# A two-layer encoder trunk on one core: layer norms with one mean operation, scaled weights, and separate output tiles for the last blocks

## The chip, the cores and the metric

The kernel runs on one core of one Trainium2 chip. The core has a matrix engine (TensorE, PE in the rows, with PEld for its weight loads), a vector engine (VectorE, DVE), a scalar engine (ScalarE, ACT), a general engine (GpSimd, POOL) and an engine that issues most transfers (SyncE, SP). Each takes its own list of instructions; they wait for one another by semaphores. The metric is device microseconds of one execution. Three runs of the kernel before took 2295.4, 2296.66 and 2297.1 us.

## What is computed

Two layers over 1024 rows (tokens) of 1024 numbers in float32. Layer 0 mixes tokens by latent attention, layer 1 by differential attention; each layer then has a gated feed-forward part:

```
h = LN(ALPHA*h + mixer(h))
h = LN(ALPHA*h + (silu(h@Wg) * (h@Wu)) @ Wd)

LN(z) = (z - mean(z)) * (mean((z-mean(z))**2) + 1e-5)**-0.5 * g + b     # per row of 1024
```

With `D = 1024` and `q` the sum of the squared distances from the mean, the norm's factor `(q/D + eps)**-0.5` is `sqrt(D) * (q + D*eps)**-0.5`, and `sqrt(D)` is 32. So the same result comes from the plain sum of squares if `g` holds 32 times its values.

## The kernel before

The rows are worked on in eight blocks of 128 (`tb` 0 to 7), one row per partition. Products are made in split precision: each operand is a high and a low part, and three matrix products replace one. The high part is a cast on ACT, the low part a subtraction on DVE or GpSimd (`split`, L480 and L481; `op_...` are weights so prepared). Inside the feed-forward parts the products are arranged in seven sub-products over halves of the operands instead of eight, which is where the many sums on DVE come from.

The order is as follows: projections and attention of layer 0, its output projection (`out_proj`), feed-forward 0 (`ffn`), projections and attention of layer 1, its output projection (class `OutProj`: begun in the attention, finished by `rest`), feed-forward 1. The instructions stand in the program in one order. A planner in the framework turns them into one list per engine: it simulates the program with costs of its own and gives a free engine the ready instruction that stands earliest in the program. `tc.high_priority(n)` moves a stretch of the program up by n places. `behind(i, j)` fixes that `i` stands after `j` in the list of their engine. The engines then run those lists as they are, so a plan that took a transfer for faster than it is makes the engine wait at that place. Buffers come from pools: the tag `big` has five buffers of 128 x 2 x 1024 numbers, handed out in turn for weights, partial sums and results, and a sixth user waits for one to come free. The tag `small` has 22 little ones for per-row values.

There are 32 layer norms, one for each block at four places, all made by `layer_norm` (L163):

- L166 and L167 (DVE) make minus the mean twice, once divided by 32, from two partial sums of the row.
- L170 (ACT) squares the two halves of `z/32 - mean/32` into a bank that is no longer needed, and adds them up (`ssq`).
- L176 (DVE) writes `y = (z - mean) * g`.
- L178 (DVE) adds the two sums and epsilon, L180 (GpSimd) raises to the power -0.5, and L183 (DVE) writes `y = y*rs + b`, followed by the store to memory (L184).

In most places `y` is `z` itself, so that L176 overwrites what L170 reads and has to wait for it. Only `out_proj` gives its last block a tile of its own:

```python
if tb == LAST_ORDER[-1]:
    y = big_tile(f"y_{nm}", F32)[:, 0]
```

The blocks of the output projections go in the order `LAST_ORDER`, 6 7 4 5 2 3 0 1. After each block's norm, `raw_x` (L440) transposes the block before it on PE (rows `xTp_a`) and makes its operands for the feed-forward part. For the last block that call is `pending()`, which `ffn` makes under `high_priority(40)` after its first gate products (`ga`). These, and the preparing of their weights (`op_gp` from `gp`, later `op_g` from `gr`), come after `rest` in the program and fill PE around that place.

The weights `g` and `b` of a norm are loaded once for a place, spread to all partitions, by transfers that GpSimd issues: `mg` and `mb` in `out_proj`, `gb` in `rest` (L424), `fg` and `fb` in `ffn` (L152), and for blocks 0 to 3 of feed-forward 0 a second pair `gb_f` (L896). They reach the queue long before the first norm that uses them.

At the end of feed-forward 1, the eleven steps of the last sub-product ("t4") run for blocks 0 and 1 together, then for 2, then for 3 (`dw` rows on PE). `last(t)` adds a finished bank to `z` (L811) and norms it; `banks_read` lists the adds. The norm of block 3 writes its last line in two halves. Blocks 4 to 7 have been normed earlier (`finish(4 + t, ...)`).

Of the kernel before, what the change touches and what calls it, by code (L numbers as in the profile page):

```python
# [9 lines left out]
F32 = mybir.dt.float32  # L10
F32R = mybir.dt.float32r
AF = mybir.ActivationFunctionType
ALU = mybir.AluOpType
# [3 lines left out]
P = 128  # L17
S = 1024
D = 1024
# [11 lines left out]
LN_EPS = 1e-5  # L31
# [11 lines left out]
def trunk(  # L43
# [66 lines left out]
    def big_tile(name, dt=F32R):  # L110
        return big.tile([P, 2, 1024], dt, tag="big", name=name)
# [13 lines left out]
    def small(name, n=1):  # L125
        return sp.tile([P, 2], F32, tag="small", name=name, bufs=22)[:, :n]
# [35 lines left out]

    def layer_norm(z, sums, junk, y, g, b, name, dst, n=1):  # L163

        nmu = small(f"nmu_{name}", 2)
        V.tensor_scalar(nmu[:, 0:1], sums[:, 0:1], sums[:, 1:2], -1.0 / (32 * D), ALU.add, ALU.mult)  # L166
        V.tensor_scalar(nmu[:, 1:2], sums[:, 0:1], sums[:, 1:2], -1.0 / D, ALU.add, ALU.mult)  # L167
        ssq = small(f"ssq_{name}", 2)
        squares = [
            A.activation(  # L170
                junk[i], z[:, i * 512:(i + 1) * 512], AF.Square,
                bias=nmu[:, 0:1], scale=1.0 / 32, accum_out=ssq[:, i:i + 1],
            )
            for i in range(2)
        ]
        centred = V.scalar_tensor_tensor(y, z, nmu[:, 1:2], g, ALU.add, ALU.mult)  # L176
        ve = small(f"ve_{name}")
        V.tensor_scalar(ve, ssq[:, 0:1], ssq[:, 1:2], LN_EPS, ALU.add, ALU.add)  # L178
        rs = small(f"rs_{name}")
        scaled = G.tensor_tensor(rs, ve, mhalf[:, 0:1], ALU.pow)  # L180
        for i in range(n):
            c = slice(i * D // n, (i + 1) * D // n)
            V.scalar_tensor_tensor(y[:, c], y[:, c], rs, b[:, c], ALU.mult, ALU.add)  # L183
            nc.sync.dma_start(dst[:, c], y[:, c])  # L184
        return squares[0].ins, centred.ins, scaled.ins

    def to_xT(y, xT, tb, name, where):
        hf, c = tb // 4, (tb % 4) * P
# [89 lines left out]
    def out_proj(side, w_o, o_dram, x_src, x_dst, lng, lnb, xo):  # L278


        with tc.tile_pool(name="op0", bufs=2, side=side, reuse_waits="tile") as pool:
            g = bcast_row(pool, lng, D, "mg0", "g")
            b = bcast_row(pool, lnb, D, "mb0", "b")
            wo = []
            for h in range(H):
                dst = ()
                if h in (0, 1, 2, 3, 7):
                    t = big_tile(f"wo0_{h}")
                    dst = (t[:, 0], t[:, 1])
                elif h == 6:  # L290
                    t = pool.tile([P, 2, D], F32R, tag=f"wo{h}", name=f"wo0_{h}", bufs=1)
                    dst = (t[:, 0], t[:, 1])
                wo.append(load_w(w_o[h], 1024, f"wo0_{h}", *dst))
            prev = None
            for tb in LAST_ORDER:
                nm = f"a0_{tb}"
                of = pool.tile([P, H, P], F32, tag="of", name=f"of_{nm}", bufs=2)
                src = o_dram[tb // 2][:, :, (tb % 2) * P:(tb % 2) * P + P]
                nc.sync.dma_start(of, src.rearrange("h p q -> p h q"))
                ot = pool.tile([P, 2, D], F32R, tag="oh", name=f"oh_{nm}").rearrange("p a (h q) -> p a h q", h=H)  # L300
                oh, ol = ot[:, 0], ot[:, 1]
                A.copy(oh, of)
# [14 lines left out]
                if tb == LAST_ORDER[-1]:  # L317
                    y = big_tile(f"y_{nm}", F32)[:, 0]
                layer_norm(z, sums, junk, y, g, b, nm, x_dst[tb * P:(tb + 1) * P, :])
                if prev is not None:  # L320
                    raw_x(prev[1], xo, prev[0], f"a0_{prev[0]}")
                prev = (tb, y)
        return lambda: raw_x(prev[1], xo, prev[0], f"a0_{prev[0]}")

    class OutProj:
# [95 lines left out]
        def rest(self, lng, lnb, xo):  # L421
            gb = big_tile("gb1", F32)
            for i, src in enumerate((lng, lnb)):
                nc.gpsimd.dma_start(gb[:, i], src.partition_broadcast(P))  # L424
            prev = None
            for tb in LAST_ORDER:
                if tb not in LAST_ORDER[:2]:
                    self.of(tb)
                if tb != LAST_ORDER[0]:
                    self.late(tb)  # L430
                z = self.z[tb]
                layer_norm(z, self.sums[tb], [self.m[tb, nh] for nh in range(2)], z, gb[:, 0], gb[:, 1],
                           f"a1_{tb}", self.x_dst[tb * P:(tb + 1) * P, :])
                if prev is not None:
                    raw_x(self.z[prev], xo, prev, f"a1_{prev}")
                prev = tb
            self.st.close()
            return lambda: raw_x(self.z[prev], xo, prev, f"a1_{prev}")

    def raw_x(y, xo, tb, name):  # L440

# [55 lines left out]
    def ffn(side, xo, xst, pending, layer, x_src, x_dst, lng, lnb, next_x, spare=()):  # L497
# [365 lines left out]

        x4 = accumulators("v", "x")
        whole(x4, from_h(6, "3"), block(1, hi_half, "b22"), True)
        for t in range(4):
            added(0, hi_half, x4[t], t, 1)
            finish(4 + t, [x4[t], x4[t]])
# [4 lines left out]

        def last(t):
            added(1, lo_half, y4[t], t, 0)
            finish(t, [y4[t], y4[t]])

        new, rest, normed = None, [], []
        if next_x is None:
            hs, ws = [], []  # L880
# [618 lines left out]
```

## Time and profile before

| | us |
|---|---|
| median of three runs | 2296.66 |
| profiled execution | 2296.31 |
| span of its instructions | 2294.4 |
| PE busy | 2249.9 (98%) |
| DVE busy | 1562.8 (68%) |
| ACT busy | 1017.9 (44%) |
| GpSimd busy | 864.8 (38%) |
| transfers, mean of 16 engines | 33.6% on the queue that SP issues to |

A row of the timeline has start, duration, engine, line, operation, output<-inputs by the program's names without buffer numbers, shape, count, and in brackets the idle time ahead of it and who ended it. A row of the waits has total, times and longest. Where the rows are the busy times of a stretch, they have each engine's busy time with the number of instructions in brackets, then the clock that PE was granted, the share of transfer time and the rate. `L183` is line 183 of the kernel. A matrix product's end is modelled, so the time from start to start (0.23 us for 512 columns here) says more than its duration.

### The profile page before, as it was taken

How to read it: one execution, taken by the hardware profiler on the slowest of the kernel's cores; microseconds unless marked ns; L12 is line 12 of the kernel's file. 1: busy time of each engine (PE TensorE's matmuls, PEld its weight loads, DVE VectorE, ACT ScalarE, POOL GpSimd, SP SyncE). 2: the span in 40 equal slices, each digit the busy share in tenths (PEclk: the TensorE clock that was granted, in tenths of full speed). 3: DMA queues.
4: the chain of work that ended last, by engine and by line, in shares of the span. 5: the costliest groups of instructions: out<-in, count | busy, mean ns of one | idle time of the engine just before them, and what ended most of it. 6: DMA issues, size and time to landing. Idle time of an engine off the chain costs nothing.

```text
span 2294.4 us, 31183 instructions
## 1 busy us (share of the span) xinstructions
PE 2249.9 (98%) x11410; PEld 1915.7 (83%) x11410; DVE 1562.8 (68%) x2899; ACT 1017.9 (44%) x2096; POOL 864.8 (38%) x688
## 2 busy tenths in 40 slices
PE   8999999999999999999999999999999999999997
PEld 8899997878888887888888888987778888887886
DVE  5667664696666668667476667676677666658777
ACT  4455573342333334445465656555432233324353
POOL 2232241114444445555432424221014444436564
PEclk9999999999999999999999999999999999999999
DMA  5010125334435338454310212054244232337353
GB/s 201 14 34 31 41 72 181 136 130 145 177 132 198 125 114 326 184 188 156 102 47 24 66 37 70 19 211 144 96 170 154 72 125 82 130 123 304 141 205 121
DMA packets 105545, 288.28 MB, mean 126 GB/s; under 512 B 7968, under 2 KB 30112, under 8 KB 94896
## 3 DMA queue, kind: packets, MB, share of 16 engines
q1 hardware_dynamic: 100976, 275.87, 33.6%
q0 software_dynamic: 4416, 10.42, 1.6%
q8 instruction: 90, 1.47, 0.3%
q14 instruction: 63, 0.52, 0.1%
HBM read 205.00 MB, written 77.07 MB: 123 GB/s over the span
## 4 chain that ended last, share of the span: by engine, by line
PE 88%; DVE 6%; DMA 3%; issue 2%; ACT 1%; POOL 1%; SPq 0%; DVEq 0%; POOLq 0%; ACTq 0%
PE gb L526 14%; PE gc L526 10%; PE ga L526 10%; PE dw L795 6%; PE zp_a L394 4%; PE s_a L216 4%; PE s_b L216 3%; PE dx L795 3%; PE dv L795 3%; PE bp L143 3%; PE bp L144 3%; PE bp L145 3%; PE dy L795 3%; PE o_a L255 2%; PE o_b L255 2%
## 5 line engine op out<-in xcount | busy, mean ns | idle before, releaser
L480 ACT CAST op_g<-gr 128x512 fp32r<-128x512 f32 x240 | 146.9, 621 | 370.8 <-PE gb L526 183.3
L481 POOL TENSOR_TENSOR op_g<-gr,op_g 128x512 fp32r<-128x512 f32 x104 | 146.4, 1413 | 248.2 <-ACT op_g L480 142.7
L481 DVE TENSOR_TENSOR op_h<-rh,op_h 128x512 fp32r<-128x512 f32 x154 | 163.8, 1091 | 63.4 <-ACT op_h L480 63.4
L526 PE MATMUL ga<-xh_m,op_g 128*128 128x512 f32 x512 | 168.1, 389 | 0.0
L480 ACT CAST op_h<-rh 128x512 fp32r<-128x512 f32 x154 | 92.9, 619 | 136.6 <-PE dx L795 36.1
L795 PE MATMUL dw<-op_w_t,op_h 128*128 128x512 f32 x660 | 151.4, 390 | 0.1
L795 PEld LDWEIGHTS dw<-op_w_t,op_h 128*128 128x128 f32 x660 | 123.6, 188 | 26.0 <-DVE op_h L481 0.5
L222 ACT ACTIVATE l_b<-l_b,mx_b 128x256 f32<-128x256 f32 (+7 forms) x128 | 99.5, 778 | 79.7 <-DVE mx_b L219 77.6
L1303 POOL TENSOR_SCALAR l_b<-l_b,r_b,cst 128x128 f32<-128x128 f32 (+3 forms) x64 | 52.8, 825 | 204.6 <-DVE r_b L224 194.0
L795 PE MATMUL dx<-op_w_b,op_h 128*128 128x512 f32 x528 | 122.2, 391 | 6.8 <-ACT op_w_b L480 3.9
L481 POOL TENSOR_TENSOR op_w_t<-tt,op_w_t 128x512 fp32r<-128x512 f32 x66 | 98.6, 1497 | 79.6 <-ACT op_w_t L480 77.8
L795 PEld LDWEIGHTS dx<-op_w_b,op_h 128*128 128x128 f32 x528 | 98.6, 188 | 30.1 <-ACT op_w_b L480 4.7
L481 DVE TENSOR_TENSOR op_g<-gr,op_g 128x512 fp32r<-128x512 f32 x136 | 110.8, 819 | 15.6 <-ACT op_g L480 15.3
L526 PE MATMUL gb<-t4h_f,op_g 128*128 128x512 f32 x352 | 115.9, 390 | 3.4 <-DVE tmp L609 3.4
L481 POOL TENSOR_TENSOR op_g<-s,op_g 128x512 fp32r<-128x512 f32 x40 | 54.3, 1358 | 167.9 <-ACT op_g L480 159.6
L526 PE MATMUL gb<-t2h_f,op_g 128*128 128x512 f32 x352 | 115.6, 390 | 0.4 <-DVE op_g L481 0.4
L526 PE MATMUL gc<-t1h_f,op_g 128*128 128x512 f32 x352 | 115.4, 389 | 0.0
L526 PE MATMUL gc<-b22h_f,op_g 128*128 128x512 f32 x352 | 115.3, 389 | 0.0
L526 PE MATMUL gb<-t3h_f,op_g 128*128 128x512 f32 x352 | 115.2, 389 | 0.0
L526 PEld LDWEIGHTS ga<-xh_m,op_g 128*128 128x128 f32 x512 | 96.1, 188 | 19.9
L143 PE MATMUL bp<-xT_f,h_wb 128*128 128x512 f32 x256 | 103.0, 402 | 0.0
L145 PE MATMUL bp<-xT_f,l_wb 128*128 128x512 f32 x256 | 101.6, 397 | 0.0
(378 smaller groups left out, 6753.9 us busy)
## 6 DMA issues: line engine op xcount, KB each, us to landing
gr<-in_w_gu SPq DMA_DIRECT2D x44, 1024.0 KB, 6.9
rh<-h_dr SPq DMA_DIRECT2D x28, 1024.0 KB, 4.8
h_dr<-sh SPq DMA_DIRECT2D x22, 1024.0 KB, 5.1
h_dr<-hp SPq DMA_DIRECT2D x22, 768.0 KB, 4.1
tt<-in_w_dn SPq DMA_DIRECT2D x22, 512.0 KB, 7.9
rh<-h_dr SPq DMA_DIRECT2D x14, 768.0 KB, 4.3
wo_dr<-op_pwo SPq DMA_DIRECT2D x16, 512.0 KB, 3.4
z<-xs_dr SPq DMA_DIRECT2D x16, 512.0 KB, 10.0
```

Of the source, the lines that this page charges most:

```text
L143: T.matmul(ps_out, lh, rh, start=(i == 0), stop=False)
L144: T.matmul(ps_out, lh, rl, start=False, stop=False)
L145: T.matmul(ps_out, ll, rh, start=False, stop=(i == n - 1))
L216: T.matmul(s[:, :w], lh, rh[:, ks], start=(j == 0), stop=(j == len(q_pass) - 1))
L222: A.activation(l[:, :n], l[:, :n], AF.Exp, bias=mx, scale=-1.0, accum_out=sm)
L255: T.matmul(po[:, c], a, b[:, j % 2, c], start=st, stop=sp_, skip_group_check=True)
L394: T.matmul(m, a[:, h, :], self.wo[h][w][:, c], start=(start and h == heads[0] and a is oh and w == 0), stop=(stop and h == heads[-1] and a ...
L480: A.copy(hi, src)
L481: return eng.tensor_tensor(lo, src, f32(hi), ALU.subtract).ins
L526: T.matmul(o, w[:, a, kc], x[b][:, k, :], start=(first and k == 0 and (a, b) == (0, 0)), stop=(k == 3 and a == 1), skip_group_check=True,)
L795: T.matmul(o, h[:, a, c], w[:, b_], start=(first and (a, b_) == (0, 0)), stop=(last and a == 1), skip_group_check=True,)
L1303: G.tensor_scalar(l1[:, :n], l1[:, :n], r1, nlam, ALU.mult, ALU.mult)
```

## The change

Three things are changed.

1. In `layer_norm` the mean is made once, undivided by 32. The squares are of `z - mean`, epsilon is multiplied by 1024, and `g` must hold 32 times its values: the new `scale_g` multiplies it in place on ACT (128 x 1024), once at each of the four places where a `g` is loaded. In the program this stands ahead of the first norm there. `layer_norm` also returns its last DVE instruction.
2. In `rest` the last block (1) writes its norm into a `big` tile of its own, and the whole norm of that block stands under `high_priority(40)`. `raw_x` reads that tile.
3. At the end of feed-forward 1 the last four blocks write their norms into two `big` tiles, two blocks each. For blocks 2 and 3, the add of the finished bank to `z` is fixed behind the last DVE instruction of the norm before it.

```diff
     def layer_norm(z, sums, junk, y, g, b, name, dst, n=1):
 
-        nmu = small(f"nmu_{name}", 2)
-        V.tensor_scalar(nmu[:, 0:1], sums[:, 0:1], sums[:, 1:2], -1.0 / (32 * D), ALU.add, ALU.mult)
-        V.tensor_scalar(nmu[:, 1:2], sums[:, 0:1], sums[:, 1:2], -1.0 / D, ALU.add, ALU.mult)
+        nmu = small(f"nmu_{name}")
+        V.tensor_scalar(nmu, sums[:, 0:1], sums[:, 1:2], -1.0 / D, ALU.add, ALU.mult)
         ssq = small(f"ssq_{name}", 2)
         squares = [
             A.activation(
                 junk[i], z[:, i * 512:(i + 1) * 512], AF.Square,
-                bias=nmu[:, 0:1], scale=1.0 / 32, accum_out=ssq[:, i:i + 1],
+                bias=nmu, scale=1.0, accum_out=ssq[:, i:i + 1],
             )
             for i in range(2)
         ]
-        centred = V.scalar_tensor_tensor(y, z, nmu[:, 1:2], g, ALU.add, ALU.mult)
+        centred = V.scalar_tensor_tensor(y, z, nmu, g, ALU.add, ALU.mult)
         ve = small(f"ve_{name}")
-        V.tensor_scalar(ve, ssq[:, 0:1], ssq[:, 1:2], LN_EPS, ALU.add, ALU.add)
+        V.tensor_scalar(ve, ssq[:, 0:1], ssq[:, 1:2], D * LN_EPS, ALU.add, ALU.add)
...
-            V.scalar_tensor_tensor(y[:, c], y[:, c], rs, b[:, c], ALU.mult, ALU.add)
+            done = V.scalar_tensor_tensor(y[:, c], y[:, c], rs, b[:, c], ALU.mult, ALU.add)
             nc.sync.dma_start(dst[:, c], y[:, c])
-        return squares[0].ins, centred.ins, scaled.ins
+        return squares[0].ins, centred.ins, scaled.ins, done.ins
+
+    def scale_g(g):
+        A.activation(g, g, AF.Copy, scale=float(math.sqrt(D)))
...
# out_proj
+                if prev is None:
+                    scale_g(g)
                 layer_norm(z, sums, junk, y, g, b, nm, x_dst[tb * P:(tb + 1) * P, :])
...
# OutProj.rest
-                z = self.z[tb]
-                layer_norm(z, self.sums[tb], [self.m[tb, nh] for nh in range(2)], z, gb[:, 0], gb[:, 1],
-                           f"a1_{tb}", self.x_dst[tb * P:(tb + 1) * P, :])
+                z = y = self.z[tb]
+                last = tb == LAST_ORDER[-1]
+                if prev is None:
+                    scale_g(gb[:, 0])
+                if last:
+                    y = big_tile(f"y_a1_{tb}", F32)[:, 0]
+                with tc.high_priority(40 if last else 0):
+                    layer_norm(z, self.sums[tb], [self.m[tb, nh] for nh in range(2)], y, gb[:, 0], gb[:, 1],
+                               f"a1_{tb}", self.x_dst[tb * P:(tb + 1) * P, :])
                 if prev is not None:
-                    raw_x(self.z[prev], xo, prev, f"a1_{prev}")
-                prev = tb
+                    raw_x(prev[1], xo, prev[0], f"a1_{prev[0]}")
+                prev = (tb, y)
...
# ffn
         whole(x4, from_h(6, "3"), block(1, hi_half, "b22"), True)
+        scale_g(g)
         for t in range(4):
...
         def last(t):
             added(1, lo_half, y4[t], t, 0)
-            finish(t, [y4[t], y4[t]])
+            if t % 2 == 0:
+                ys.append(big_tile(f"y_{nm}_{t}", F32))
+            if t > 1:
+                behind(banks_read[-1], normed[-1][3])
+            normed.append(finish(t, [y4[t], y4[t]], ys[-1][:, t % 2]))
...
+            scale_g(gb[:, 0])
             whole(y4, from_h(2, "4", ("o",)), t4(), False)
```

More of the change, by code (lines that the diff above doesn't have):

```diff
@@ L430, in rest @@
                     self.late(tb)
-                z = self.z[tb]
-                layer_norm(z, self.sums[tb], [self.m[tb, nh] for nh in range(2)], z, gb[:, 0], gb[:, 1],
-                           f"a1_{tb}", self.x_dst[tb * P:(tb + 1) * P, :])
+                z = y = self.z[tb]
[7 more added lines that the diff above has]
+                               f"a1_{tb}", self.x_dst[tb * P:(tb + 1) * P, :])
                 if prev is not None:
-                    raw_x(self.z[prev], xo, prev, f"a1_{prev}")
-                prev = tb
+                    raw_x(prev[1], xo, prev[0], f"a1_{prev[0]}")
+                prev = (tb, y)
             self.st.close()
-            return lambda: raw_x(self.z[prev], xo, prev, f"a1_{prev}")
+            return lambda: raw_x(prev[1], xo, prev[0], f"a1_{prev[0]}")
     def raw_x(y, xo, tb, name):
@@ L875, in last @@
             added(1, lo_half, y4[t], t, 0)
-            finish(t, [y4[t], y4[t]])
+            if t % 2 == 0:
[3 more added lines that the diff above has]
+            normed.append(finish(t, [y4[t], y4[t]], ys[-1][:, t % 2]))
         new, rest, normed = None, [], []
         if next_x is None:
-            hs, ws = [], []
+            hs, ws, ys = [], [], []
             for h, w in zip(from_h(2, "4", late=True), t4()):
```

## The prediction

> **What bounds the kernel now.** I read the page first: busy shares and the chain that ended last.
>
> ```profile
> span 2294.4 us, 31183 instructions
> ...
> PE 2249.9 (98%) x11410; PEld 1915.7 (83%) x11410; DVE 1562.8 (68%) x2899; ACT 1017.9 (44%) x2096; POOL 864.8 (38%) x688
> ...
> PE 88%; DVE 6%; DMA 3%; issue 2%; ACT 1%; POOL 1%; SPq 0%; DVEq 0%; POOLq 0%; ACTq 0%
> ```
>
> TensorE (PE) is busy for 2249.9 of 2294.4 us and is 88% of the chain. No layer norm can give back more than PE's idle 44.5 us, and only the part of it that a norm causes. The profiled execution took 2296.31 us (1.9 us lie around its span), 0.35 us below the median of the runs, 2296.66. So I next read who makes PE wait.
>
> ```profile
> PE xTp_a L148 <- DVE z_a L183: 2.1, 1, 2.1
> ...
> PE xTp_f L148 <- DVE y_f L183: 0.8, 1, 0.8
> ```
>
> (Columns: total us, times, longest.) Of all of PE's waits these two alone name a norm's last line, L183. The first belongs to the last block of `OutProj.rest`, which the change edits. What it costs beside the wait is in the busy times by stretch (PE first; PEclk is the granted clock, third from the end):
>
> ```profile
> core 0: us, PE busy (x) PEld busy (x) DVE busy (x) ACT busy (x) POOL busy (x), PEclk, DMA share, GB/s
> 353.00:357.00 4.00, 4.00 (x13) 3.32 (x13) 1.23 (x1) 2.13 (x4) 0.00 (x0) 0.51 1.04 399
> ...
> 1644.00:1646.70 2.70, 0.64 (x3) 0.19 (x1) 2.26 (x5) 1.59 (x3) 0.93 (x1) 1.00 0.80 256
> 1646.70:1651.00 4.30, 4.27 (x16) 3.70 (x17) 1.96 (x3) 2.10 (x5) 0.00 (x0) 0.60 1.01 390
> ```
>
> After the wait PE ran 4.30 us at a granted clock of 0.60, which is 0.40 x 4.30 = 1.72 us lost behind it. The wait is worth 2.09 + 1.72 = 3.81 us.
>
> **The change, part by part.**
>
> *One mean operation.* 32 norms (two per layer, eight blocks each) lose L167, a 0.2 us instruction that follows L166 by 0.12 us (the two rows at 1639.56 and 1639.68 below). That is 3.8 us of VectorE (DVE) in all, hidden where PE is busy; cover gone, it counts 0.12 us per exposed norm. I take 0.1 us at the second wait above; in the two chains below it is already left out.
>
> *The wait in `rest`.* The timeline of its last block, all engines:
>
> ```profile
> 1639.56 0.20 DVE L166 TENSOR_SCALAR nmu_a<-sum_a 128x1 f32<-128x1 f32 x1
> 1639.68 0.21 DVE L167 TENSOR_SCALAR nmu_a<-sum_a 128x1 f32<-128x1 f32 x1
> 1639.80 2.02 DVE L481 TENSOR_TENSOR op_gp<-gp,op_gp 128x512 fp32r<-128x512 f32 x2
> ...
> 1641.34 0.19 ACT L170 ACTIVATION_READ_ACCUMULATOR zp_a<-z_a,nmu_a 128x1 f32 x1
> ...
> 1642.95 1.27 DVE L176 SCALAR_TENSOR_TENSOR z_a<-z_a,nmu_a,gb 128x1024 f32<-128x1024 f32 x1
> 1644.15 0.20 DVE L178 TENSOR_SCALAR ve_a<-ssq_a 128x1 f32<-128x1 f32 x1
> ...
> 1645.39 1.29 DVE L183 SCALAR_TENSOR_TENSOR z_a<-z_a,rs_a,gb 128x1024 f32<-128x1024 f32 x1 [0.44 <-POOL rs_a L180]
> ...
> 1646.73 1.61 PE L148 MATMUL xTp_a<-ident,z_a 128*128 128x128 f32 x8 [2.09 <-DVE z_a L183]
> ...
> 1647.52 0.69 DVE L459 TENSOR_TENSOR xr_m<-xTp_a,xr_m 128x512 f32<-128x512 f32 x1 [0.25 <-PE xTp_a L148]
> ...
> 1649.55 0.69 DVE L481 TENSOR_TENSOR op_gp<-gp,op_gp 128x512 fp32r<-128x512 f32 x1 [1.33 <-ACT op_gp L480]
> ...
> 1651.29 0.69 DVE L557 TENSOR_TENSOR gr<-gr 128x512 f32<-128x512 f32 x1 [1.05 <-DMA gr<-in_w_gu]
> ```
>
> In place, L176 cannot overwrite `z` while ScalarE's (ACT's) squares read it; meanwhile DVE takes other work (2.02 us of `op_gp`, two adds of `raw_x`), so L178 comes 2.6 us after the squares end (1641.53 against 1644.15). With `y` in its own tile and 40 places of priority L176 follows L166 at once (to about 1641), and L178 waits only for the squares: 1641.55, or 0.67 later behind one foreign operation. L178 to L183 took 1.24, L183 takes 1.29: done at 1644.1 to 1644.7. PE's work ahead of the transposes ends at 2.09 before 1646.73, that is 1644.64. The wait shrinks to at most 0.1. What is late next: DVE's first `gr` work, which waits for a DMA until 1651.29. Nothing in the change brings that load sooner; the new tile even takes one of the five `big` buffers, and a load that wants one may have to wait for it. Ends: nothing gained (DVE's following stretch stays pinned to that load, and PE meets it later) and 3.81 gained. I take the DVE idle time that the earlier norm can fill before that load, 0.25 + 1.33 + 1.05 = 2.63 (its three waits between 1646.6 and 1651.3): **-2.6 us**.
>
> *The clock rule.* The row above gives 0.60 after 2.09 us of waiting. [...]
>
> *The end.* The last four blocks, from the timeline:
>
> ```profile
> 2269.75 12.85 PE L795 MATMUL dw<-wt,op_h 128*128 128x512 f32 x55 [0.73 <-POOL wt L481]
> ...
> 2273.80 0.69 DVE L811 SCALAR_TENSOR_TENSOR z<-z,dw 128x512 f32<-128x512 f32 x1
> ...
> 2277.56 0.21 DVE L178 TENSOR_SCALAR ve_f<-ssq_f 128x1 f32<-128x1 f32 x1
> ...
> 2278.28 0.21 DVE L166 TENSOR_SCALAR nmu_f<-fs 128x1 f32<-128x1 f32 x1
> ...
> 2283.51 0.68 DVE L811 SCALAR_TENSOR_TENSOR z<-z,dw 128x512 f32<-128x512 f32 x1
> ...
> 2284.11 1.28 DVE L176 SCALAR_TENSOR_TENSOR z<-z,nmu_f,fg 128x1024 f32<-128x1024 f32 x1
> ...
> 2285.43 0.20 DVE L166 TENSOR_SCALAR nmu_f<-fs 128x1 f32<-128x1 f32 x1
> ...
> 2285.67 0.69 ACT L170 ACTIVATE dw<-z,nmu_f 128x512 f32<-128x512 f32 x1 [2.21 <-DVE nmu_f L166]
> ...
> 2287.14 0.19 ACT L170 ACTIVATION_READ_ACCUMULATOR dw<-z,nmu_f 128x1 f32 x1
> ...
> 2288.57 0.21 DVE L178 TENSOR_SCALAR ve_f<-ssq_f 128x1 f32<-128x1 f32 x1
> ...
> 2289.44 1.41 DVE L183 SCALAR_TENSOR_TENSOR z<-z,rs_f,fb 128x512 f32<-128x512 f32 x2 [0.66 <-POOL rs_f L180]
> ```
>
> A block alone takes: add 0.60, L166 to squares 0.24, squares 1.66, 0.03 to L178, 0.87 to L183, L183 1.2: 4.6 us. The last one needed 5.93 from add to L183 because block 2's L176 stood between. Separate tiles take 5.93 to 3.4. But `behind` now holds block 2's add until block 1's L183, and block 3's until block 2's; queued behind each are all later DVE instructions. Block 1's L166 also came only after block 0's L178 (2277.56, 2278.28), though its add ran at 2273.80, so norms don't overlap much. New sum: block 1's add 2273.80, block 0's L166 0.60 later at 2274.40, its L178 2276.33, block 1's L166 2276.5, its squares to 2278.4, its L178 behind block 0's L183 at 2279.0, its L183 2279.87, done 2281.08; block 2's add there, block 3's 4.61 later at 2285.69, its L183 at 2289.09 against 2289.44: **-0.35 us**. Ends: +1.0 (block 0's L183 goes ahead of block 1's L176, half a microsecond per pair) and -3.2 (block 3's add when PE ends, 2269.75 + 12.85 = 2282.6, then 3.4).
>
> *Scaling `g`.* Four new 128x1024 ACT operations, none in the trace; the nearest row is a cast of that size, 1.05 us. Each also waits for its load, and with it whatever stands behind it on ACT, as ACT stood for 0.98 us at 347.36. Where it stands in ACT's order decides:
>
> ```profile
> 343.62 0.59 POOL L152 DMA_DIRECT2D mg<-in_ln_mix_g  x1
> ...
> 344.89 1.05 ACT L136 CAST wo<-r_wo 128x1024 fp32r<-128x1024 f32 x1
> ...
> 347.36 1.04 ACT L302 CAST oh_a<-of_a 128x1024 fp32r<-128x1024 f32 x1 [0.98 <-DMA of_a<-o_dr]
> ```
>
> ```profile
> mg<-in_ln_mix_g POOLq DMA_DIRECT2D x1, 512.0 KB, 5.9
> ...
> gb<-in_ln_mix_g POOLq DMA_DIRECT2D x1, 512.0 KB, 8.5
> ```
>
> ```profile
> 1504.66 0.59 POOL L424 DMA_DIRECT2D gb<-in_ln_mix_g  x1 [4.52 <-PE s_b L216]
> ```
>
> ```profile
> 1509.79 0.27 ACT L243 CAST pth_b<-pt_b 128x128 fp32r<-128x128 f32 x1 [1.76 <-DVE ptl_b L244]
> ...
> 1521.53 1.15 ACT L222 ACTIVATE l_b<-l_b,mx_b 128x1024 f32<-128x1024 f32 x1 [2.66 <-DVE mx_b L219]
> ```
>
> ```profile
> 1000.00:1050.00 50.00, 50.00 (x222) 41.42 (x221) 38.84 (x52) 26.27 (x52) 30.76 (x25) 1.00 0.56 204
> ```
>
> Layer 0: `mg` lands at 349.5, at the end of attention. Ends 0 (a later gap holds it) and 3.2 us (ahead of the cast at 347.36, which would start at 350.55); I take half an operation and a little, 0.6, as for a place near the landing. Layer 1: `gb` lands at 1513.2. Ends 0 (in the 2.66 us gap ahead of 1521.53) and 4.4 (in the 1.76 us gap ahead of 1509.79, which would then start at 1514.2); I take 0.5, since the wide gap lies behind the landing. The two `fg` of `ffn` land while the last gate products run and the first down weights are loaded: 0 to one wait like the 1.76 each, 0.2 together, because PE waits for those weights there anyway. The fourth, `gb_f`, comes while PE is 50.00 of 50 us busy (last row): 0, and 1.05 if that cover went. Together **+1.3 us**, 0 to 12.
>
> **Sum.** -2.6 - 0.35 - 0.1 + 1.3 = -1.75: 2294.6 for the profiled execution, 2294.9 for the median.
>
> **Rivals.** *The whole wait goes and the scaling is free:* -3.81 - 0.35 - 0.1 = -4.3, and -7 with the best end: 2292.4 to 2289.5. For it: in layer 0 the last block already has its own tile, and its transposes appear in no wait row. Against: it needs four operations to fall into gaps.
>
> *Slower: the scaling in `rest` holds ACT at the end of layer 1's attention.* Planned into the gap before 1509.79, it makes those casts 4.4 late, PE waits as long, and the clock drops as at 353 (0.51 for 4.00 us, 2 us lost): 6.4 + 0.8 for the other scalings - 3.05 = +4.2 and, with `mg` at its end too, +6.8: 2301 to 2303.5. It decides if the planner counts less than about 5 us from the issue at 1504.66. For it: this landing took 8.5 us and that of `mg`, as large, 5.9. Against: ACT has wider gaps later.
>
> *It doesn't do what it says:* `rest`'s norm is earlier but PE meets the `gr`-bound DVE work later: -0.45 + 1.3 = +0.9, 2297.5.
>
> *The slow clock isn't the wait's doing:* only 2.09 is to be had in `rest`: -1.2, 2295.4. [...]
>
> **How the numbers follow.** Forecast 0.42, free scaling 0.18, held ACT 0.20, given back 0.14, clock 0.06. A change of 0.2% (4.6 us) is about what can be told from none. Faster by more: 0.14 of the free-scaling case and 0.02 of the others' re-planned orders, 0.16. Slower by more: 0.16 of the held case and 0.02, 0.18. Same 0.66. The range 2290.8 to 2303.5 reaches into both outer cases and leaves 0.1 on each side; the forecast's own is 2293 to 2297.
>
> **What would show it.** Right: no wait of `xTp_a` for L183, clock 1.00 in the 4 us behind; L176 beside the squares in the last blocks, the last add near 2285.7 minus what PE gained; four 1.05 us ACT rows on `g`. Wrong: ACT rows waiting for `mg`, `gb` or `fg`, new PE waits behind them, or a longer PE wait near the first `op_g` products.

## The result, and the profile after

The kernel after took 2301.61 us (median of 10 runs, 2299.70 to 2303.91), the kernel before beside it on the same chip 2295.34 us (10 runs, 2293.19 to 2297.90). The ratio is 1.0026, 95% interval 1.0018 to 1.0035: slower by 6.3 us. The forecast was 2294.9 us and no change that can be told; the measured time lies inside the range given, where the rival with the scaling that holds ACT put it (2301 to 2303.5).

The page of after, and TensorE's waits in it (total us, times, longest):

```profile
span 2298.8 us, 31151 instructions
...
PE 2252.2 (98%) x11410; PEld 1919.2 (83%) x11410; DVE 1559.4 (68%) x2867; ACT 1021.8 (44%) x2101; POOL 864.2 (38%) x688
...
PE 92%; DVE 4%; ACT 2%; DMA 1%; issue 1%; POOL 1%; SPq 0%; DVEq 0%; POOLq 0%; ACTq 0%
```

```profile
PE dx L806 <- ACT op_w_b L491: 5.8, 2, 2.9
...
PE o_b L258 <- ACT pth_b L246: 2.8, 1, 2.8
PE xTp_a L148 <- DVE y_a L183: 2.1, 1, 2.1
...
PE gb L537 <- DVE tmp L616: 1.2, 1, 1.2
PE zp_a L399 <- ACT zp_a L170: 1.0, 1, 1.0
```

Two of these waits as they are before:

```profile
PE dx L795 <- ACT op_w_b L480: 3.9, 2, 1.9
...
PE o_b L255 <- ACT pth_b L243: 0.3, 1, 0.3
```

DVE lost 3.4 us of work and 32 instructions (the forecast had 3.8 us and 32), and no gain is to be seen from it. Four things are to be seen in the waits. The wait of `xTp_a` that was to go is there, still 2.1 us. `o_b` waits 2.8 us for a cast of `pth_b` (0.3 us before). The first wait of `dx` in each ffn is 2.90 us where it was 1.95. And two waits of about 1 us are new, one for the squares of a norm of `rest` (`zp_a`) and one for DVE in the first gates (`gb`).

*Where the time went.* I cut both spans at the same instructions of TensorE, those behind waits that both kernels have, and subtract. Each span is that of a single run; these two differ by 4.4 us, the medians by 6.3. The two that matter most, from the timelines of TensorE (before, then after):

```profile
1511.05 0.63 PE L148 MATMUL pt_b<-ident,l_b 128*128 128x128 f32 x4 [1.28 <-DVE l_b L1304]
...
1557.64 0.44 PE L148 MATMUL pt_b<-ident,l_b 128*128 128x128 f32 x2 [1.92 <-DVE l_b L1304]
...
1700.15 0.50 PE L526 MATMUL gb<-t4h_f,op_g 128*128 128x512 f32 x1 [1.36 <-DVE tmp L609]
```

```profile
1509.59 0.63 PE L148 MATMUL pt_b<-ident,l_b 128*128 128x128 f32 x4 [1.28 <-DVE l_b L1321]
...
1559.97 0.44 PE L148 MATMUL pt_b<-ident,l_b 128*128 128x128 f32 x2 [1.91 <-DVE l_b L1321]
1562.76 4.38 PE L399 MATMUL zp_a<-wo,oh_a 128*128 128x512 f32 x18 [0.96 <-ACT zp_a L170]
...
1702.77 0.50 PE L537 MATMUL gb<-t4h_f,op_g 128*128 128x512 f32 x1 [1.27 <-DVE tmp L620]
```

The end of layer 1's attention takes 1559.97 - 1509.59 = 50.38 us, and took 46.59: +3.79. From there to 1700 it is 142.80 against 142.51. The other stretches, cut in the same way at the waits named (us):

| stretch of TensorE | before | after | slow cells, before / after |
|---|---|---|---|
| start to 33 (`cp`) | 33.26 | 32.05 | 0 / 0 |
| 33 to 505 (first `gb` wait) | 472.54 | 471.91 | 2 / 2 |
| 505 to 1095 (ffn 0, to `xTp_f`) | 590.19 | 590.60 | 0 / 1 |
| 1095 to 1511 (layer 1 to `pt_b`) | 415.06 | 415.03 | 0 / 0 |
| 1511 to 1557 (end of attention) | 46.59 | 50.38 | 0 / 1 |
| 1557 to 1646 (`rest`, to `xTp_a`) | 89.09 | 88.31 | 1 / 0 |
| 1646 to 1700 (first gates) | 53.42 | 54.49 | 1 / 1 |
| 1700 to 2268 (ffn 1, to `dw`) | 567.91 | 568.12 | 0 / 1 |
| 2268 to the end of the span | 26.34 | 27.91 | 0 / 1 |

The last column counts stretches at a low clock, which the next paragraph explains. Outside 1511 to 1557 much of the difference goes with it, and the experiments had to separate the two.

*A clock that goes by a grid.* In all 14 profiles of this case TensorE's granted clock is 1.00 or 0.50. Within one profile the slow stretches begin at whole multiples of 3.413 us from each other (in after at 873.78, 1515.48, 1648.60 and 2071.86: 188.00, 39.00 and 124.00 times 3.413 apart), and most last one such cell (3.413 us at 0.50 in the clock records of after's trace), that is 1.71 us of full speed lost; at 349 there are two in a row in 11 of the 14 profiles, and once two at 1559. The busy times in three cells of before and two of the kernel with the last tiles alone (below), whose `xTp_a` waits nearly as long, 2.04 us:

```profile
1643.74:1647.15 3.41, 1.32 (x8) 0.82 (x8) 2.97 (x5) 1.59 (x3) 0.93 (x1) 1.00 0.82 271
1647.15:1650.56 3.41, 3.41 (x13) 2.92 (x11) 1.51 (x3) 1.66 (x4) 0.00 (x0) 0.50 0.98 383
1650.56:1653.98 3.42, 3.42 (x16) 2.79 (x16) 2.69 (x5) 3.42 (x7) 0.00 (x0) 1.00 0.67 265
```

```profile
1640.88:1644.29 3.41, 1.77 (x8) 1.13 (x6) 2.97 (x5) 1.59 (x3) 0.93 (x1) 1.00 0.96 303
1644.29:1647.70 3.41, 3.01 (x18) 2.63 (x19) 2.33 (x5) 2.49 (x5) 0.00 (x0) 1.00 0.99 400
```

(Columns: PE busy, PEld, DVE, ACT, POOL, then the granted clock.) Above, the whole wait fell into one cell, TensorE was busy for 1.32 of 3.41 us, and the next cell ran at 0.50. Below, the edge of a cell cut the wait, the first part left 1.77 us busy, and the clock stayed at 1.00. I counted this for all cells of the 14 profiles that ran at full clock, from 30 us on and without the end of TensorE's work: busy for less than half of the cell, the next one was slow in 46 of 51 (below 0.42 in every one); 0.5 to 0.6, in 12 of 43; 0.6 to 0.8, in 0 of 118. So the wait of about 2 us at `xTp_a` lost 1.71 us of full speed behind it in before and nothing with the last tiles alone, by where the grid lay in that run.

Over the timed runs the mean granted clock is 0.9947 for before (33 runs) and 0.9931 for after (10): 0.0016 x 2295 = 3.7 us more of full speed is lost. That doesn't make 3.7 of the 6.3 us, for a slow cell can lie where TensorE would have waited anyway (the test behind `dx` below). Nor are clock and waits separate causes: the first waits of `dx`, 1.95 us each, have no slow cell behind them in before, and at 2.90 us each has one in after.

### The profile page after: what moved, and what is told of

Read it like the earlier page. It is cut to its first block, busy times and chain, and to the rows that moved or that the text cites. A ratio compares the mean times of both kernels' runs of the same rounds, so it can differ in the third digit from the quotient of the medians.

```text
span 2298.8 us, 31151 instructions
## 1 busy us (share of the span) xinstructions
PE 2252.2 (98%) x11410; PEld 1919.2 (83%) x11410; DVE 1559.4 (68%) x2867; ACT 1021.8 (44%) x2101; POOL 864.2 (38%) x688
## 4 chain that ended last, share of the span: by engine, by line
PE 92%; DVE 4%; ACT 2%; DMA 1%; issue 1%; POOL 1%; SPq 0%; DVEq 0%; POOLq 0%; ACTq 0%
PE gb L537 15%; PE gc L537 10%; PE ga L537 10%; PE dw L806 7%; PE dx L806 5%; PE zp_a L399 4%; PE s_a L219 4%; PE s_b L219 3%; PE dv L806 3%; PE dy L806 3%; PE bp L144 3%; PE bp L143 3%; PE bp L145 3%; PE o_a L258 2%; PE o_b L258 2%; PE hq L1017 1%
```

## The experiments

The times of twelve kernels are compared with runs of before on the same chip (medians of 2294.93 to 2295.47 us). The differences given are those of the medians; the ratios aren't quotients of these medians and stray from them by up to 1 us. The interval of a ratio is about 0.0009 to either side, 2 us, so a difference below that is read from the stretches of the profile, not from the median. A profile is one run, and not always one near the median: that of `rest`'s tile alone took 2300.84 us (median 2297.13), that of the last tiles alone 2292.65 (median 2294.81).

**The three parts alone.**

*The norm alone*: one mean, and the four scalings.

```
-        nmu = small(f"nmu_{name}", 2)
-        V.tensor_scalar(nmu[:, 0:1], ..., -1.0 / (32 * D), ALU.add, ALU.mult)
-        V.tensor_scalar(nmu[:, 1:2], ..., -1.0 / D, ALU.add, ALU.mult)
+        nmu = small(f"nmu_{name}")
+        V.tensor_scalar(nmu, sums[:, 0:1], sums[:, 1:2], -1.0 / D, ALU.add, ALU.mult)
...
+                if prev is None:
+                    scale_g(gb[:, 0])
```

> The kernel before with the one-mean norm and the four scalings of g alone; the tiles of rest and of the last blocks stay as before. Held ACT (main theory: the scaling of gb waits 3.10 us for its load at 1511.71 in the trace of after, and PE then waits 2.83 us): a like wait of o_b for pth_b near 1514, slow clock behind it, and +2.5 to +4.0 us against before, that is most of the 6 us. Rest theory (the load of gr comes late because y took a big buffer): within 1 us of before. Tail theory (the last blocks' tiles and order cost): within 1 us of before.

Measured: 2299.19 us, ratio 1.0021 (1.0012 to 1.0030), +4.2 us. Its stretch from 1511 to 1557 is 50.43 us, its wait of `o_b` 2.87 us, with a slow cell behind. The theory of the held ACT gave this (expected +2.5 to +4.0); the other two had expected no more than 1 us.

*`rest`'s own tile alone*, with the priority:

```
+                if last:
+                    y = big_tile(f"y_a1_{tb}", F32)[:, 0]
+                with tc.high_priority(40 if last else 0):
                     layer_norm(z, ..., y, gb[:, 0], gb[:, 1], ...)
```

> The kernel before with the own tile and the 40 places of priority in rest alone; two means, no scaling. Held ACT: 0 to +1 us against before, no new wait near 1514. Rest theory: +2.0 to +4.0 us, with gr's first DVE work 2 to 3 us later than the 1651.29 of before, and new waits of PE for gb near 1700. My prediction on record: -2.6 us, no wait of xTp_a for L183. The planned order already speaks against it: the two op_gp still stand ahead of L176 in DVE's order and the two adds of raw_x ahead of L178, so I look for xTp_a waiting about 2.1 us again. Tail theory: 0.

Measured: 2297.13 us, ratio 1.0011 (1.0002 to 1.0020), +2.1 us. `xTp_a` waits 2.04 us: the part gains nothing and loses something. Rows of all engines:

```profile
1641.04 2.02 DVE L485 TENSOR_TENSOR op_gp<-gp,op_gp 128x512 fp32r<-128x512 f32 x2
...
1642.98 1.27 DVE L176 SCALAR_TENSOR_TENSOR y_a<-z_a,nmu_a,gb 128x1024 f32<-128x1024 f32 x1
...
1645.37 0.20 DVE L178 TENSOR_SCALAR ve_a<-ssq_a 128x1 f32<-128x1 f32 x1
...
1646.62 1.28 DVE L183 SCALAR_TENSOR_TENSOR y_a<-y_a,rs_a,gb 128x1024 f32<-128x1024 f32 x1 [0.44 <-POOL rs_a L180]
...
1647.93 0.33 SPq L184 DMA_DIRECT2D xs_dr<-y_a  x1
...
1648.35 1.15 SPq L539 DMA_DIRECT2D gr<-in_w_gu  x2
...
1654.46 0.69 DVE L561 TENSOR_TENSOR gr<-gr 128x512 f32<-128x512 f32 x1 [4.38 <-DMA gr<-in_w_gu]
```

In before the first `gr` load had stood ahead of the store:

```profile
1642.23 0.43 SPq L535 DMA_DIRECT2D gr<-in_w_gu  x1
```

The priority did not move the two `op_gp` behind L176, and the two adds of `raw_x` still precede L178. New is the order on SP: the store of `y` now stands ahead of the first `gr` load and waits for L183, and the load behind it is issued at 1648.35 (1642.23 in before). DVE then waits 4.38 us for `gr`, and TensorE 2.03 us for DVE at 1699, with a slow cell behind. In after, with as many cells as the norm alone, the stretch from 1646 to 2060 is 414.47 us against 413.07: +1.40.

*The last tiles alone*:

```
-            finish(t, [y4[t], y4[t]])
+            if t % 2 == 0:
+                ys.append(big_tile(f"y_{nm}_{t}", F32))
+            if t > 1:
+                behind(banks_read[-1], normed[-1][3])
+            normed.append(finish(t, [y4[t], y4[t]], ys[-1][:, t % 2]))
```

> The kernel before with tiles of their own for the last four blocks and the two holds by behind alone; TensorE's order is that of before, instruction for instruction. Held ACT and rest theory: -0.5 to +0.3 us against before, first add to last L183 about 16.3 us. Tail theory: +1.2 to +2.0 us, with TensorE's clock below 0.8 in the 4 us behind its last wait, as in the profile of after (0.66 for 2272 to 2276).

Measured: 2294.81 us, ratio 0.9999 (0.9991 to 1.0008), -0.2 us, no slow clock behind the last wait. From there to the end of the span 26.48 us against 26.34. The 27.91 of after's profile holds a slow cell (clock 0.66 from 2272 to 2276) that the new tiles don't make: `rest`'s tile alone, whose tail is that of before, has it too (27.83).

The three parts sum to 4.2 + 2.1 - 0.2 = 6.1 of the 6.3 us, each known to about 2 us.

**The held ACT.** First, *the scaling of `gb` alone*, by 1.0, added to before:

```
+                if prev is None:
+                    A.activation(gb[:, 0], gb[:, 0], AF.Copy, scale=1.0)
```

> The kernel before with one added instruction: ACT multiplies gb by 1.0 in rest (in place of the scaling; two means, no other scaling, no new tiles). Measures the held ACT by itself. Held ACT: a wait of o_b for pth_b of about 2.8 us near 1514, the stretch between the waits of pt_b at 1511 and 1557 3.5 to 4.0 us longer than the 46.59 of before, +3.0 to +4.5 us against before. If the other scalings or the one-mean norm make most of e1_norm's +4.2 us, it is below +2 us.

Measured: 2300.99 us, ratio 1.0023 (1.0013 to 1.0032), +5.5 us. One instruction of 1.06 us makes most of the loss. In its own stretch from 1511 to 1557 it costs 3.9 us (50.50 against 46.59); the norm alone, which has the same instruction, lost 4.2, so the 5.5 isn't to be added to the other parts. The rows of after, then those of this kernel:

```profile
1503.21 0.59 POOL L429 DMA_DIRECT2D gb<-in_ln_mix_g  x1 [4.53 <-PE s_b L219]
...
1508.34 0.27 ACT L246 CAST pth_b<-pt_b 128x128 fp32r<-128x128 f32 x1 [1.76 <-DVE ptl_b L247]
1511.71 1.06 ACT L188 ACTIVATE gb<-gb 128x1024 f32<-128x1024 f32 x1 [3.10 <-DMA gb<-in_ln_mix_g]
1512.67 1.02 ACT L225 ACTIVATE l_b<-l_b,mx_b 128x896 f32<-128x896 f32 x1
1513.70 0.62 ACT L246 CAST pth_b<-pt_b 128x256 fp32r<-128x256 f32 x2
...
1514.10 0.39 PE L258 MATMUL o_b<-pth_b,bvh 128*128 128x256 f32 x1 [2.83 <-ACT pth_b L246]
```

```profile
1511.25 1.06 ACT L433 ACTIVATE gb<-gb 128x1024 f32<-128x1024 f32 x1 [3.19 <-DMA gb<-in_ln_mix_g]
1513.36 0.16 DVE L224 RECIPROCAL r_b<-sm_b 128x1 f32<-128x1 f32 x1 [3.66 <-ACT l_b L222]
...
1513.64 0.39 PE L255 MATMUL o_b<-pth_b,bvh 128*128 128x256 f32 x1 [1.80 <-ACT pth_b L243]
```

The load is issued at 1503.21 and lands 8.5 us later. ACT reaches the scaling at 1508.6, has nothing it may do in its place, and stands for 3.10 us; the exponential and the two casts behind it then start without a wait of their own. Then DVE stands for the exponential (3.66 us in this kernel), and TensorE for the cast. The expected 2.8 us of that one wait are only 1.80 here, with a slow cell over the work ahead (from 1508.70); the stretch is as long all the same.

*The scaling of `gb` moved*, in the kernel after, behind an exponential of the last head where ACT was idle:

```
-                    scale_g(gb[:, 0])
+                    behind(scale_g(gb[:, 0]), exps["b7_7_0"])
```

> The kernel after with one thing moved: the scaling of gb in rest stands behind the exponential of the last head's block 7, first map (1518.74 in the trace of after), where ACT had 3.71 us free. Held ACT: no wait of o_b for pth_b near 1514, clock 1.00 there, and 2.5 to 4 us less than after: +2 to +3.5 us against before. Rest theory and tail theory: the same as after within 1 us, +5 to +7 us against before.

Measured: 2298.32 us, ratio 1.0013 (1.0004 to 1.0022), +3.3 us, so about 3.0 of the 6.3 us are back. The stretch from 1511 to 1557 is 47.18 us (50.38 in after), and no wait for `pth_b` above 0.3 us is left (one of 1.02 us for a load of `wo` comes up in its place).

*The two scalings of `fg` moved as well*, behind the casts of the down projection's second stage:

```
-        scale_g(g)
+        behind(scale_g(g), casts[0])
```

> e4_late with the two fg scalings moved as well, behind the casts of the second stage of the down projection, so that they no longer stand ahead of the first cast of op_w_b on ACT. Clock theory: the first wait of dx falls from 2.90 to 1.95 us in both ffns, the small waits behind it come back (1.2 to 1.5 us in all), slow clock behind it in under half of the runs, and 0.5 to 1.8 us less than e4_late: +1.5 to +2.8 us against before. Wait theory: the same sum of waits, so +3.3 us as e4_late.

Measured: 2295.83 us, ratio 1.0006 (0.9998 to 1.0015), +0.8 us. The first wait of `dx` is 1.95 us again and 0.94 us comes back behind it. By stretches it gives 590.58 to 590.05 in ffn 0 and 207.96 to 207.06 in ffn 1, 1.4 us together against the kernel above; the medians differ by 2.5. Only the part in ffn 0 lies outside the spread of the other kernels (they are given at the end of the account of the prediction), so about half a microsecond is shown.

**A test of the slow clock behind `dx`.** The kernel after, with 16 transposes of the identity into the first accumulator ahead of each first down product, so that TensorE is busy in the wait (the product overwrites them):

```
+    def keep_warm(bank, n):
+        for k in range(n):
+            i = T.transpose(bank[:, :P], ident, ident).ins
+            if k == 0:
+                behind(i, last_mm[0])
...
+        keep_warm(x4[0], 16)
         whole(x4, hs, ws, True)
```

> The kernel after with 16 transposes of the identity into the first accumulator ahead of each ffn's first down product, in the 2.90 us that TensorE waits there; what they write is overwritten by the first product. Every other instruction stands in the same order on every engine but one product moved by seven places. Clock theory (cells of 3.41 us, counted through the whole run; a cell in which TensorE is busy for less than about half makes the next cell run at half clock and costs 1.71 us): no slow clock behind these two waits, first products at the same place, and 2 to 3.4 us less than after, +2.7 to +4.5 us against before. Wait theory (only the waits cost, the clock is the same lottery in both kernels): no change, +5.5 to +6.5 us against before.

Measured: 2300.67 us, ratio 1.0024 (1.0014 to 1.0034), +5.6 us. The slow cells behind `dx` are gone, and the time is not: over its nine runs the mean granted clock is 0.9949 (0.9931 in after), as high as in before, and the loss stays within the noise of the 6.3 us. Two cells of after, two of this kernel, then TensorE's rows with waits in the same order:

```profile
870.37:873.78 3.41, 0.99 (x4) 0.67 (x4) 2.55 (x4) 3.13 (x6) 1.61 (x2) 1.00 0.92 372
873.78:877.19 3.41, 3.41 (x9) 2.55 (x9) 3.38 (x3) 0.52 (x2) 2.88 (x2) 0.50 0.99 321
```

```profile
872.30:875.71 3.41, 2.26 (x18) 1.93 (x17) 2.55 (x4) 2.84 (x5) 1.31 (x2) 1.00 0.90 365
875.71:879.13 3.42, 3.42 (x15) 2.24 (x13) 3.39 (x3) 1.43 (x3) 3.20 (x2) 1.00 0.99 316
```

```profile
872.79 32.00 PE L806 MATMUL dx<-op_w_b,op_h 128*128 128x512 f32 x132 [2.90 <-ACT op_w_b L491]
```

```profile
875.01 4.20 PE L814 MATMUL dx<-op_w_b,op_h 128*128 128x512 f32 x16 [1.15 <-ACT op_w_b L499]
879.59 20.25 PE L814 MATMUL dx<-op_w_b,op_h 128*128 128x512 f32 x88 [0.38 <-DVE op_w_b L500]
900.04 6.21 PE L814 MATMUL dx<-op_w_b,op_h 128*128 128x512 f32 x26 [0.20 <-DVE op_h L500]
```

That the slow cell comes from the wait is shown: same place, same wait, filled with 1.91 us of transposes, the next cell at 1.00 and not at 0.50, no slow cell in either ffn. The transposes count as work for it: in the cell from 872.30 the products behind the wait alone, from 875.01 on, are 0.70 of the 3.41 us, and with the transposes TensorE is busy for 2.26. My theory of its price falls here. Behind `dx`, TensorE at full clock runs into its operands, and the slow cell in after stood where before has waits of 0.29 and 1.02 us. Ffn 0 takes 590.32 us filled and 590.60 unfilled: at most 0.28 of the 1.71 us was on the path. The ten kernels without a scaling ahead of that cast say the same: ffn 0 takes 589.91 to 590.45 us in the three with a slow cell behind `dx`, and 589.93 to 590.39 in the seven without. So the waits behind it took up most of this cell's 1.71 us; from 1646 to 1700 (below) one cost 1.30 to 1.67.

**The wait of `xTp_a`.** *Its store behind the load.* The kernel with `rest`'s own tile, and the store of `y` ordered behind the first `gr` load:

```
+                behind(nc.sync.dma_start(self.x_dst[prev[0] * P:(prev[0] + 1) * P, :], prev[1]).ins, loads[0])
```

> The own tile in rest without scaling and with two means, as in e2_rest, and the store of that tile ordered behind the first gr load on SP (in e2_rest it stands ahead of it and waits for L183, so the load is issued at 1648.35 and not at 1642.23). Queue theory (the store holds the load): gr's first DVE work near 1651.3 again, 3 us earlier than the 1654.46 of e2_rest, the wait of gb near 1699 at 1.4 us again, and the time that of before within 0.8 us. Buffer theory (the tile takes a big buffer and the load waits for one): the load stays late and the time is that of e2_rest, +2.1 us. xTp_a waits about 2.0 us for L183 in either.

Measured: 2294.34 us, ratio 0.9996 (0.9987 to 1.0005), -0.7 us. The load is issued at once, ahead of the store, and DVE waits 1.06 us for it:

```profile
1640.71 0.38 SPq L547 DMA_DIRECT2D gr<-in_w_gu  x1
1645.13 0.33 SPq L448 DMA_DIRECT2D xs_dr<-y_a  x1
...
1648.52 0.69 DVE L570 TENSOR_TENSOR gr<-gr 128x512 f32<-128x512 f32 x1 [1.06 <-DMA gr<-in_w_gu]
```

The stretch from 1646 to 2060 is 413.09 us, 415.93 with the store ahead (one slow cell more among it). The kernel after with its scalings moved gives the same pair: 414.03 us with the store ahead, without a slow cell, and 413.21 with the store behind the load, with one. It was the store on SP's queue; the tile takes its `big` buffer in both kernels, and the buffer cost nothing.

*Old work really kept out.* The two `op_gp` behind the last block's L183:

```
+                if layer == 1 and n == 2:
+                    behind(turns["last"], marks[LAST_ORDER[-1]][3])
```

> e5_store with one thing more: the two op_gp that stood ahead of the last block's L176 come behind its L183 on DVE. So old work is really kept out. My prediction's term: the wait of xTp_a for L183 falls from 2.0 to under 0.6 us and the time by 2.0 to 3.4 us against before. Given back: the wait goes, but the products that want op_gp and the first gr work come later, new waits of gb near 1700 add up to 1.5 to 2.5 us more, and the time is that of before within 0.8 us.

Measured: 2294.60 us, ratio 1.0000 (0.9991 to 1.0008), -0.5 us. Only the `op_gp` are kept out; the two adds still precede L178, so the norm comes 1.26 us earlier and not the full 2.09. What it gains is given back:

```profile
1643.24 1.89 DVE L493 TENSOR_TENSOR op_gp<-gp,op_gp 128x512 fp32r<-128x512 f32 x3
...
1643.38 1.09 PE L148 MATMUL xTp_a<-ident,y_a 128*128 128x128 f32 x8 [0.83 <-DVE y_a L183]
...
1644.56 14.18 SPq L554 DMA_DIRECT2D gp<-in_w_gu  x2
```

The wait is 0.83 us and its slow cell is gone. But the `gp` load on SP's queue wants the buffer that the held `op_gp` free late, products of `ga` wait 0.79 us at 1667, and `gb` still waits 1.29 at 1697. From 1557 to 1700 it takes 141.54 us with one slow cell, and `rest` with the store moved 142.00 with two: the kernel with the shorter wait is the longer one by up to 1.25 us once the cell is taken out (at 1.71 us; less where a cell costs less).

*TensorE given other work instead.* Before, with the transposes behind 24 products that wait for nothing:

```
+                if name == f"a1_{LAST_ORDER[-1]}" and kh == k == 0:
+                    behind(i, last_mm[0])
```

> The kernel before with one order changed: the transposes of rest's last block come behind the 24 products of the first two gates' second halves, which wait for nothing, so that TensorE has work while the norm ends. The wait of xTp_a for L183 goes to 0 without a faster norm, and the slow clock behind it too. If that wait is on the path: -2 to -3.5 us against before. If what follows is bound by DVE's work and the gr load (given back): new waits between 1650 and 1705, 1700 us reached no earlier than in before, within 0.8 us of it or slower.

Measured: 2293.37 us, ratio 0.9995 (0.9986 to 1.0003), -2.1 us, not told apart from none. No wait for L183 is left; waits of 0.99, 0.78, 0.60 and 0.44 us stand between 1643 and 1696 in its place, 2.81 us against 2.04 + 1.36 = 3.40 in the kernel with the last tiles alone. From 1557 to 1700 both take about the same (140.41 and 140.89, one slow cell each). So the 2 us wait itself is worth about half a microsecond in this pair of profiles. The cell behind it is worth more: 1646 to 1700 takes 51.79 us without one (the last tiles alone), 53.09 to 53.46 with one (before, and four kernels whose first `gr` load comes as early).

**All repairs, and a faster kernel.** *The whole change with its three repairs* (`gb` and `fg` scaled later, the store behind the load):

> The kernel after with all three repairs: the scaling of gb and the two of fg moved behind work on ACT where nothing waits (as in e8_fg) and the store of rest's own tile behind the first gr load on SP (as in e5_store). If held ACT and the store on SP are the whole loss, nothing of the 6 us is left: the first gr work 2.5 to 3.5 us earlier than in e8_fg, 1.0 to 2.2 us less than e8_fg, -1.5 to +0.5 us against before. If something else of the change costs (the one-mean norm, the last tiles), it stays above +1.0 us.

Measured: 2294.87 us, ratio 0.9998 (0.9989 to 1.0007), -0.6 us. The whole loss is gone, and what the change was to bring does not appear either.

*Busy through the waits.* The kernel of the moved transposes, with idle transposes of the identity at the ends of the two attentions:

```
+            if name == f"a{H - 1}_1" and j == 1:
+                warm = keep_warm(ps_s("warm"), 10, i)
...
+            if name == f"b{H - 1}_1":
+                keep_warm(pt, 11, last_pv[f"b{H - 1}_1"])
```

> e10_xtp with transposes of the identity in two waits of TensorE at the ends of the two attentions: ten in the 1.6 us before o_a's product near 349 (into a bank of their own) and eleven in the 1.9 us before the transposes of pt_b near 1557 (into the bank that these overwrite). Clock theory: the slow cells behind 349 (two in a row, 2 to 3 us lost in every profile) and behind 1557 (1.71 us lost in 7 of 11) go, the stretch from 349 to 505 is 153.5 to 155.0 us instead of 155.8 to 157.0, and since TensorE bounds what follows both, the time is 2.5 to 5 us under that of before. If slow cells are absorbed by later waits here too, as those behind dx were in e7_fill, it is that of e10_xtp, within 1 us.

Measured: 2291.50 us, ratio 0.9982 (0.9973 to 0.9991), -3.4 us: faster than both kernels. Its profile holds one slow cell up to TensorE's end (before four, after seven). The mean granted clock of its runs is 0.9966 (before beside it 0.9947; 0.0018 unrounded): 0.0018 x 2295 = 4.1 us of full speed won back, enough for the whole gain. The kernel of the moved transposes alone had -2.1 us (-3.2 to +0.7), so what the idle transposes add to it isn't told from noise. The expectation was met only in part. At 349 a wait that had been split became one, and the cell stayed:

```profile
346.41 1.25 PE L148 MATMUL warm<-ident 128*128 128x128 f32 x10
348.22 0.39 PE L266 MATMUL o_a<-pth_a,vh 128*128 128x256 f32 x1 [0.56 <-ACT pth_a L254]
...
350.61 0.39 PE L266 MATMUL o_a<-ptl_a,vh 128*128 128x256 f32 x1 [1.78 <-DVE ptl_a L255]
...
1554.16 1.39 PE L148 MATMUL pt_b<-ident 128*128 128x128 f32 x11
...
1558.77 3.51 PE L411 MATMUL zp_a<-wo,oh_a 128*128 128x512 f32 x14 [1.62 <-ACT zp_a L179]
```

33 to 505 takes 471.69 us, no less than in the two other profiles with a single slow cell there (471.51 and 471.77; with two it is 471.83 to 473.01). At 1557 the order changed besides: products of `zp_a` now run ahead of the last transposes of `pt_b`. The gain is therefore shown for the kernel, and its clock for the whole, but it is not shared out between the three places, and that the clock is its cause is likely, not shown.

## Why the prediction was wrong, by its own steps

*The scaling of `gb`: +0.5, with ends 0 to 4.4.* Two steps failed: this one, which makes most of the loss, and the wait in `rest` below, which missed its forecast by more. The sum had -1.75 and the kernel took +6.3, 8.0 us apart: about 3.3 here (3.8 for 0.5) and 4.7 there (+2.1 for -2.6). The scaling measured +3.8 us in its stretch, and +5.5 us (3.0 to 7.3) as a kernel. I took the low end because ACT had a gap of 2.66 us behind the landing. But the place in ACT's order was set from an estimate of when the load lands, and the row at hand said that the estimate mattered: issue at 1504.66, 8.5 us to land. The rival of the held ACT had the mechanism and the load time; it put the scaling ahead of the cast at 1509.79, and it stood right behind it, ahead of an exponential. Its price was off: 6.4 us for this place where 3.8 were measured, less 3.05 of gains in `rest` and elsewhere that didn't come. That the time lies in its 2301 to 2303.5 is in part luck, two errors that cancel. What it needed, a planner that counts less than about 5 us for a load of 8.5, fits the order that came out (what the planner counted isn't on record), and nothing in my text had a row against it. Idle time of ACT elsewhere was no argument: an instruction in a fixed order can't use it, and ACT stood for 3.10 us.

*The wait in `rest`: -2.6.* This step failed in three parts. The 40 places of priority moved neither the two `op_gp` nor the adds, so the wait stayed at 2.09 us (the step had at most 0.1). The store in the same block was moved, though, ahead of the `gr` load on SP, and that cost 1.40 us from 1646 to 2060 in after and 2.84 in the kernel with the tile alone, a slow cell among the latter; the prediction looked for this cost in the `big` buffer, which was innocent. And the price was wrong even for a change that does it: with the wait cut to 0.83 us, or to none, the time stays within the noise of before. The rival "it doesn't do what it says" saw that nothing would be gained here, and gave +0.9 for the whole change; the tile alone was +2.1.

*The slow clock: 1.72 us for each wait as seen.* The size was exact (1.71), its certainty was not. Of the four profiles in which a wait of about 2 us stands at `xTp_a` in before's order of work (before, the norm alone, the last tiles alone, `gb` alone) three had the cell. The rival that gave it no part in the wait falls: the filled waits of `dx` have no slow cell, the cell behind the first at 1.00 (0.50 in after). The sum should have held a chance for each wait, in both kernels, and whether something waits behind it.

*The end: -0.35, ends +1.0 and -3.2.* Right within what can be told: -0.2 us (-2.1 to +1.8), 26.48 us against 26.34. The order came as worked out, but the 0.35 us didn't: from the first add to the last L183 it is 2277.45 to 2293.83, 16.38 us in after and 16.32 before. From an add to its mean took 0.73 us where the block stood alone, and the sum had taken 0.60 from rows in which other work lay between.

*The norm of one mean: -0.1.* 3.4 us of DVE's time went, and no stretch shows it; a term of 0.1 us can't be told.

*The other scalings: `mg` 0.6, two `fg` 0.2, `gb_f` 0.* With `gb` these are five new operations, not four, since `fg` is scaled in both ffns; the sum had them all. `mg` shows nothing (33 to 505 is 471.9 us, within the spread of the others). `gb_f` waited 5.7 us for its load on ACT with TensorE busy, and cost nothing, as forecast. The two `fg` cost about 0.4 in ffn 0 (590.60, 590.52 and 590.58 with the scaling ahead of the cast, 589.91 to 590.45 without); in ffn 1 the spread of the others (207.06 to 208.09 from 2060 to 2268) covers it. That is more than 0.2, for TensorE waits there for the very cast that stands behind the scaling on ACT: the cover that the step named, a wait for the weights, was the path.

## What to carry to other kernels

An instruction that waits for a load belongs behind everything ready on its engine; how long the load takes to land (8.5 us here), not how idle the engine is, says whether it may stand in a chain that ends a stage. When a block of work is moved, follow each of its instructions onto its own queue: here the store, not the arithmetic, went first and held a load. A wait is worth its length only if what follows is not waiting as well (the one of 2 us at `xTp_a` was worth about 0.5), and here a wait of about 2 us brought a slow cell of 1.71 us or none. The one kernel that was clearly faster gave TensorE other work in its waits; shortening a wait gave nothing that can be told.

## What was not expected of the hardware

The time of a run goes with the clock granted, and that, by the profiles, with how the grid lies (3.413 us cells, a slow one after 46 of 51 cells less than half busy, and none after 118 cells busy for 0.6 to 0.8): 33 runs of before on one chip spread from 2292.84 to 2298.38 us, one cell is 1.71, and the eleven runs at a mean clock of 0.994 took 2295.84 us on average, the nineteen at 0.995 2294.76. Single profiles hold one to eight slow cells (before four, the last tiles alone, with the same order on TensorE, three, `rest`'s tile alone eight, and the kernel kept busy one), so a single pair of them can show a loss or a gain of several microseconds that isn't the change's. Between 0.42 and 0.6 busy the same share went both ways, and what decides there stays open.
